# New ranks and later landings in the planner that writes a hybrid decoder layer's instruction order

## The chip, the cores and the metric

The kernel runs on one core of a Trainium2 chip. The metric is the device time in microseconds (us) from the start to the end of one execution; several executions are timed and the median is given. Five engines work beside each other: TensorE (PE in the profile), VectorE (DVE), ScalarE (ACT), GpSimd (POOL) and SyncE (SP), which issues nearly all transfers. Each engine works through its own instructions in the order in which they are written; waits between engines go over semaphores.

## The reference

One layer over 4096 tokens of width 1024, in float32. The input is normalised, scaled and shifted by a conditioning vector, and goes through one input projection that feeds three groups of heads; their gated outputs are joined, projected, normalised and added to the input:

```python
h = _rmsnorm(x, g_pre) * (1.0 + scale[:, None]) + shift[:, None]
proj = h @ w_in
aq, ak, av, ag, rkv, rg, gq, gkk, gv, gg = jnp.split(proj, ...)
attn = _sliding_window_attention(aq, ak, av, sinks) * silu(ag)      # 8 heads, window 128, sinks, ALiBi
rwkv = _rwkv7_mixer(h, rr, rk, rv, ...) * silu(rg)                  # 4 heads, a state of 64 x 64 each
gla  = _gla_mixer(h, gq, gkk, gv, ...) * silu(gg)                   # 4 heads, a state of 32 x 64 each
y = jnp.concatenate([attn, rwkv, gla], axis=-1) @ w_out
return x + gate[:, None] * _rmsnorm(y, g_post)
```

The RWKV group is a recurrence over tokens, `S = S*w + sa*(kk*a) + v*k`, with `sa = -S@kk`. In chunks of 64 tokens it needs, for each chunk and head, the inverse of a triangular 64 x 64 matrix.

## The kernel before

The tokens go in 16 tiles of 256. The work has two phases with a handover between them. Every projection is made of three float16 products (high by high, high by low, low by high parts).

In the first phase each tile passes these stages, whose names are the keys of `LAG`:

- `a` loads and normalises the tile and splits it into `hT` (also stored to DRAM for the second phase);
- `p` makes its projections, PSUM tiles `pv`, `lp`, `zz` (keys, receptances, values) and `gqk`, in a tag `pj` of two banks, and evicts them, `zz` by ACT into `zs` and by DVE into `zb`;
- `w` (the function `stage_d`) makes decays and gates, with `zp`, `gp`, `wps`, `aps`;
- `qa` normalises keys (`np`), makes the products `KB` and `RA` on DVE, the chunk matrices `atp` in PSUM and `AT`, and stores their diagonal blocks of 16 x 16 to DRAM (`adr`);
- `qb` reads them back as `AS`, inverts them row by row on DVE in 15 pairs of `tsc` and `TT`, stores the result (`tdr`) and reads it back as `td` by eight transfers;
- `qc` widens the inverse to 64 x 64 by four bursts of small matmuls (`Xp`, `Xq`, `Xp`, `X2`, the last shown as `X`) into `tf`;
- `v` transposes values (`vp`) and makes the bonus (`bp`); `k` transposes `KB` (`kp`, two bursts) into `BK`;
- `q2` runs the recurrence over the tile's four chunks (`rp`, `up`, `sp`, `yp`) and normalises its output (`ysb`, `yt`);
- `r` is the GLA group (`ktp`, `gap`, `kvp`, `op`, `ot`).

Three further stages run beside them: `l` splits the first phase's weights k, r, v and gqk at the start; `c` reads the second phase's weights piece by piece (`cs`), splits them (`ch`) and stores them to DRAM; `g` makes the output gate.

The second phase has `s` (attention: scores `sc`, softmax, `ovp`), `m` (joins and scales the three groups and splits them into blocks `mtp`) and `p2` (queries, keys and values `qp`, `kp`, `vp`; gates `gp`; and the seven products `op` of the output projection, in a scheme of sums of blocks, whose weights `o` stay in SBUF or come as `ov`). The handover (loads of the second phase's weights, the first tile's attention, the first projections) is written between the phases, outside the planner's lists.

The order is made in two steps. First the stages are generators, run by `emit()` with a coarse model of time: this fixes the program order, the tiles and the buffers. Second, `Order.note` records for each instruction an engine, a modelled duration `occ`, a modelled time to its result `lat`, and what it needs; and `Order.pin`, called once for each phase, is a list scheduler: for the engine that is free first it takes, among the steps that are ready by the model, the one with the lowest `rank`, and ties the engine's instructions together in that order. A rank is the step's number in program order plus an offset:

```python
st.half, st.rank = None, len(self.steps) + self.lag
...
self.model.order.lag = LAG.get(self.model.stage, 0) - self.model.order.urgent
```

`urgent` is 150 around evictions of the second phase (`URGENT`) and 0 in the first. On PE a step of another array shape than the one in use is taken only when no step of that shape is ready, or after it has waited 0.6 us where the shape in use is the full one. A transfer's data are ready `lat` after its issue starts, or later where a shared pipe of 400 GB/s says so.

Of the kernel before, what the change touches and what calls it, by code (L numbers as in the profile page):

```python
# [31 lines left out]
HOP, VL, AL, PL = 0.4, 0.2, 0.2, 0.06  # L32
EXP_TABLE, LN_TABLE = 1, 2
LIFT = {}
LAG = {"l": 150}
URGENT = 150
HOME = {('kp', 'mq'): 'tr', ('cw', 'm'): 'at'}
TILING_WAIT = 0.6
# [27 lines left out]
class Order:  # L66
# [34 lines left out]
    def note(self, eng, name, outs, ins, func, r):  # L101

        st = Step()
# [3 lines left out]
        e, o = st.eng, outs[0]  # L107
# [3 lines left out]
        if e == "PE":  # L111
            f32, lhs = ins[0].dtype == F32, self.region(ins[0])
            n = math.prod(o.shape[1:])
            _, p0, p1, _ = self.region(o)
            rows, cs = (lhs[1] // 32, (lhs[2] + 31) // 32), (p0 // 32, (p1 + 31) // 32)
            rows, cs = [(0, 4) if b - a > 2 else (a, b) for a, b in (rows, cs)]
            mode = (rows[1] - rows[0], cs[1] - cs[0])
            took = n * (2 if f32 else 1) / 2400 + 0.003
            took = max(took, 0.056 if not f32 else 0.0 if mode[1] < 4 else 0.109 if n > 16 else 0.21)
            issue = 0.017 if f32 and mode == (1, 2) else 0.009 if f32 and mode[0] == 1 else 0.007  # L120
            cells = [4 * a + b for a in range(*rows) for b in range(*cs)]
            st.array = (mode, cells, 2 if f32 and name == "matmul" else 1, took, issue)
            st.occ = st.lat = 0.0
        elif e == "SP":
            st.bytes = math.prod(ins[0].shape) * SIZE[ins[0].dtype]
            kb = st.bytes / 1024
            st.occ = 0.47
            st.lat = next((t for k, t in ((8, 2.0), (32, 2.2), (128, 2.8), (256, 3.7), (512, 4.6)) if kb <= k), 5.2)
        elif e == "Activation":
            st.occ = (0.05 if on_psum else 0.093) + 0.093 * (len(ins) - 1) + 0.832e-3 * n  # L130
            st.lat = st.occ + 0.1
            if len(outs) > 1:
                st.occ += 0.187
                st.lat = st.occ + 0.02
            st.table = LN_TABLE if func == AF.Ln else EXP_TABLE if func in (AF.Exp, AF.Tanh) else None
        elif e == "Pool":
            if name == "memset":
                st.occ = 0.06
            elif name == "tensor_copy":
                st.occ = 0.25 if n <= 2 else 0.11 + 0.95e-3 * n  # L140
            elif n <= 8:
                st.occ = 0.33 + 0.165 * n
            else:
                st.occ = 0.42 + 1.5e-3 * n if n <= 512 else 1.85e-3 * n
            st.lat = st.occ + 0.05
        else:
            if name == "tensor_reduce":
                n = math.prod(ins[0].shape[1:])
            fast = name in ("tensor_scalar", "tensor_single_scalar") and not on_psum and o.dtype == F32
            fixed, rate = 0.065 + 0.06 * (cols > 0), 1.04e-3  # L150
            if fast:
                rate = 0.53e-3
            elif name == "transpose":
                fixed = 0.09
            elif name == "tensor_tensor_scan":
                rate = 2.08e-3
            elif name == "memset":
                fixed, rate = 0.05, 0.3e-3
            elif name == "tensor_tensor" and len(o.shape) == 3 and o.shape[2] <= 16 and n > 16:
                fixed, rate = 0.09, 1.55e-3  # L160
            st.occ = fixed + rate * n
            st.lat = st.occ + 0.085
# [70 lines left out]
    def pin(self):  # L233
# [22 lines left out]
        while count < len(steps):  # L256
            e = min((e for e in ENGINES if ready[e]), key=lambda e: max(free[e], min(ready[e].values())))
            now = max(free[e], min(ready[e].values())) + 1e-9
            at = sorted((k for k, t in ready[e].items() if t <= now), key=lambda k: (steps[k].rank, k))
            k = at[0]  # L260
            if e == "PE" and mode is not None and steps[k].array[0] != mode:

                same = [q for q in at if steps[q].array[0] == mode]
                wait = max(now - ready[e][q] for q in at if steps[q].array[0] != mode)
                if same and (mode != (4, 4) or wait < TILING_WAIT):
                    k = same[0]
            if steps[k].port and held > now + SWAP:
                k = next((q for q in at if not steps[q].port), k)
            first = max(free[e], ready[e].pop(k))
            for k in bursts.get(k, [k]):  # L270
                st, t = steps[k], max(first, free[e])
                if e == "PE":
                    m, at, passes, took, issue = st.array
                    if mode is not None and m != mode:
                        t = max(t, max(cells)) + 0.094
                    mode = m
                    t = max(t, max(cells[c] for c in at))
                    for c in at:
                        cells[c] = t + passes * took
                    free[e], st.end = t + issue * passes, t + passes * took + 0.165  # L280
                else:
                    if st.half is not None:
                        was, half[e] = half.get(e, st.half), st.half
                        if was[0] != st.half[0] or None not in (was[1], st.half[1]) and was[1] != st.half[1]:
                            t = max(t, free[e] + 0.115)
                    if st.table is not None and st.table != table:
                        t, table = max(t, free[e] + 1.28), st.table
                    if st.port:
                        t = max(t, held)
                        held = t + st.occ  # L290
                    free[e], st.end = t + st.occ, t + st.lat
                    if st.bytes:

                        pipe = max(pipe, t + 1.7) + st.bytes / 400e3
                        st.end = max(st.end, pipe)
                st.start = t
                if e in last:
                    self.tc.add_manual_dep(
                        st.ins, last[e], mybir.DependencyInfo(mybir.DependencyClass.NoSync, mybir.DependencyReason.DATA))
                last[e], count = st.ins.name, count + 1  # L300
                for q in st.then:
                    to, h = steps[q], head[q]
                    left[h] -= 1
                    at = t if k in to.turn else 0.0
                    if k in to.needs and e != to.eng:
                        at = max(at, st.end + HOP_FROM[e] + HOP_INTO.get(to.eng, 0.0))
                    elif k in to.needs and (e == "SP" or e != "PE" and to.needs[k]):
                        at = max(at, st.end + (0.05 if e == "SP" else 0.03))
                    when[h] = max(when[h], at)
                    if not left[h]:  # L310
                        ready[to.eng][h] = when[h]
# [27 lines left out]
class Lane:  # L339
# [6 lines left out]
    def __getattr__(self, name):  # L346
        f = getattr(self.eng, name)

        def call(*args, **kw):
# [7 lines left out]
            self.model.order.behind = self.model.gate if self.model.stage in ("c", "g") else None  # L357
            self.model.order.lag = LAG.get(self.model.stage, 0) - self.model.order.urgent
            self.model.order.note(self.eng, name, aps[:1] + ([] if accum is None else [accum]),
# [1852 lines left out]
```

## Time and profile before

| what | value |
|---|---|
| median of 3 runs | 1984.49 us (1982.57 to 1984.66) |
| the profiled execution | 1984.65 us, span 1982.8 us |
| PE busy | 1878.0 us (95%) |
| DVE busy | 1425.1 us (72%) |
| ACT busy | 1111.7 us (56%) |
| POOL busy | 369.9 us (19%) |
| granted TensorE clock, mean | 0.989 |

The span runs from the first to the last instruction of the core; the time includes what lies around it. Nearly all instructions are recorded by one helper, so rows of the profile carry its line, L352, and are told apart by the names of what they write and read: `zb<-zz,mu_c,zs` is an instruction that writes zb and reads zz, mu_c and zs. "Idle before" is the time in which an engine did nothing before the instruction, and the name behind the arrow is what ended it. `SPq` is SP's queue of transfer issues.

### The profile page before, as it was taken

The page shows a single profiled execution, that of the slowest core. Times are in us where ns is not written, and L with a number is a line of the kernel's source. Part 1 is how long each engine was busy: PE and PEld are TensorE (multiplying, and loading weights), DVE is VectorE, ACT ScalarE, POOL GpSimd, SP SyncE. Part 2 cuts the span into 40 slices and gives each one's busy share as a digit, 9 for nine tenths or more (in the row PEclk, how much of TensorE's full clock was granted, in tenths as well). Part 3 has the DMA queues.
Part 4 walks back from the last instruction along what each step waited for, and adds up shares of the span by engine and source line. Part 5 has one row for each costly group of instructions (what it writes and reads, how often), then busy time and mean ns, then how long its engine had stood idle before and what let it go on. Part 6 is the DMA issues. An engine that isn't in the chain of part 4 may idle for free.

```text
span 1982.8 us, 59059 instructions
## 1 busy us (share of the span) xinstructions
PE 1878.0 (95%) x24651; PEld 1451.6 (73%) x24651; DVE 1425.1 (72%) x3919; ACT 1111.7 (56%) x2529; POOL 369.9 (19%) x549
## 2 busy tenths in 40 slices
PE   5889999899999999999899999999999999999997
PEld 1667778778777877787777677876778777787783
DVE  4878777887877888877657776667666676666756
ACT  4977877666776677654335443444434444344443
POOL 0623223452322444332200000000000000000001
PEclk8999999999999999999999999999999999999999
DMA  9464444443342434225244433344333434334315
GB/s 376 139 214 141 150 126 132 130 126 110 114 149 76 134 96 122 62 67 162 88 143 145 152 110 113 111 145 124 117 110 111 150 118 123 105 112 153 110 47 182
DMA packets 154261, 257.55 MB, mean 130 GB/s; under 512 B 49026, under 2 KB 100994, under 8 KB 147844
## 3 DMA queue, kind: packets, MB, share of 16 engines
q1 hardware_dynamic: 153844, 253.19, 40.0%
q8 instruction: 195, 3.19, 0.7%
q14 instruction: 78, 0.64, 0.1%
q10 hardware_dynamic: 144, 0.52, 0.1%
HBM read 192.83 MB, written 60.82 MB: 128 GB/s over the span
## 4 chain that ended last, share of the span: by engine, by line
PE 58%; DVE 19%; ACT 9%; DMA 9%; issue 3%; SPq 2%; POOL 1%; DVEq 0%; ACTq 0%; POOLq 0%
PE gp L352 17%; PE op L352 11%; PE zz L352 5%; PE qp L352 5%; PE kp L352 3%; PE pv L352 2%; PE lp L352 2%; PE ovp L352 2%; DVE mtp L352 2%; DVE q L352 2%; DMA AS<-adr 2%; PE gqk L352 2%; PE sc L352 2%; SPq L352 2%; DVE pr L352 1%
## 5 line engine op out<-in xcount | busy, mean ns | idle before, releaser
L352 PEld LDWEIGHTS <-mtp 128*128 128x128 f16 x1344 | 128.7, 98 | 143.4 <-issue 8.1
L352 ACT ACTIVATE pr<-pr,nm,lsc 128x160 f32<-128x160 f32 (+2 forms) x256 | 129.0, 506 | 100.8 <-DVE nm L352 100.8
L352 PE MATMUL op<-o,mtp 128*128 128x512 f16 x768 | 182.2, 379 | 2.6 <-DVE yv L352 2.6
L352 PE MATMUL op<-ov,mtp 128*128 128x512 f16 x576 | 142.2, 379 | 3.1 <-DMA ov<-woscr 2.4
L352 PEld LDWEIGHTS <-hT 128*128 128x128 f16 x1536 | 120.3, 99 | 31.4 <-issue 8.1
L352 DVE SCALAR_TENSOR_TENSOR ag<-ag,gp 128x512 f32<-128x512 f32 x64 | 43.9, 686 | 136.9 <-ACT ag L352 136.9
L352 ACT ACTIVATE ag<-gp,gh 128x512 f32<-128x512 f32 x64 | 43.9, 686 | 156.9 <-PE gp L352 156.8
L352 POOL TENSOR_TENSOR ry<-sy,expo 128x1 f32<-128x1 f32 x30 | 17.7, 608 | 582.9 <-DVE sy L352 582.9
L352 DVE TENSOR_TENSOR yv<-op,yv 128x512 f32<-128x512 f32 x105 | 72.2, 689 | 60.5 <-PE op L352 41.1
L352 PE MATMUL pv<-gvh,hT 128*128 128x272 f16 x512 | 99.5, 288 | 12.8 <-DVE zb L352 6.6
L352 PE MATMUL zz<-hT,rh 128*128 128x256 f16 x512 | 93.9, 277 | 0.4 <-DVE zb L352 0.3
L352 PE MATMUL zz<-hT,kh 128*128 128x256 f16 x512 | 90.7, 274 | 0.0
L352 DVE CUSTOM_DVE_ANT_0 pr<-sc,ab,kept 128x160 f32<-128x160 f32 (+2 forms) x256 | 83.2, 375 | 10.4 <-PE sc L352 10.2
L352 PE MATMUL lp<-hT,Lh 128*128 128x256 f16 x512 | 90.6, 273 | 0.1
L352 PE MATMUL zz<-hT,vh 128*128 128x256 f16 x512 | 89.5, 274 | 0.0
L352 PE MATMUL gp<-hT,q4h 128*128 128x256 f16 x512 | 87.8, 273 | 1.6 <-issue 1.6
L352 PE MATMUL gqk<-hT,gqkh 128*128 128x256 f16 x512 | 88.4, 274 | 0.8 <-DVE zb L352 0.8
L352 PE MATMUL gp<-hT,q3h 128*128 128x256 f16 x512 | 86.7, 273 | 0.0
L352 PE MATMUL qp<-hT,q0h 128*128 128x256 f16 x512 | 86.0, 273 | 0.0
L352 PE MATMUL qp<-hT,q1h 128*128 128x256 f16 x512 | 85.7, 272 | 0.0
L352 PE MATMUL gp<-hT,q5h 128*128 128x256 f16 x512 | 85.5, 273 | 0.0
L352 PE MATMUL gp<-hT,q6h 128*128 128x256 f16 x512 | 85.0, 273 | 0.0
(429 smaller groups left out, 5723.1 us busy)
## 6 DMA issues: line engine op xcount, KB each, us to landing
ov<-woscr SPq DMA_DIRECT2D x96, 512.0 KB, 4.1
xh<-in_x SPq DMA_DIRECT2D x32, 512.0 KB, 4.0
xt<-in_xc SPq DMA_DIRECT2D x16, 1024.0 KB, 8.4
hscr<-hT SPq DMA_DIRECT2D x16, 1024.0 KB, 5.0
hT<-hscr SPq DMA_DIRECT2D x16, 1024.0 KB, 4.8
x<-in_x SPq DMA_DIRECT2D x30, 512.0 KB, 4.2
out<-yv SPq DMA_DIRECT2D x30, 512.0 KB, 2.9
cs<-in_w SPq DMA_DIRECT2D x56, 256.0 KB, 3.5
```

Of the source, the lines that this page charges most:

```text
L352: r = f(*args, **kw)
```

## The change

Three edits in the planner, none in the computation. Fourteen stages get an offset of rank, where one had it before; the modelled landings of transfers become later; and a step on SP that needs an earlier transfer's data is taken to be ready 1.2 us after that landing.

```diff
-LAG = {"l": 150}
+LAG = {"l": 150, "a": -50, "qb": -100, "qc": -200, "k": -150, "c": 170, "p": 130, "v": 130, "r": 120, "w": 60, "q2": 40, "m": -100, "p2": -80, "s": 50}
...
             st.occ = 0.47
-            st.lat = next((t for k, t in ((8, 2.0), (32, 2.2), (128, 2.8), (256, 3.7), (512, 4.6)) if kb <= k), 5.2)
+            st.lat = next((t for k, t in ((8, 2.2), (64, 3.2), (128, 3.4), (256, 4.4), (512, 5.8)) if kb <= k), 7.5)
...
                     elif k in to.needs and (e == "SP" or e != "PE" and to.needs[k]):
-                        at = max(at, st.end + (0.05 if e == "SP" else 0.03))
+                        at = max(at, st.end + (1.2 if e == "SP" else 0.03))
```

The lists of durations and the rule for array shapes stay as they are, and so do program order, tiles and buffers.

## The prediction

> **What bounds the kernel now.** I read the page's first part, then a table of five stretches of the span.
>
> ```profile
> span 1982.8 us, 59059 instructions
> PE 1878.0 (95%) x24651; PEld 1451.6 (73%) x24651; DVE 1425.1 (72%) x3919; ACT 1111.7 (56%) x2529; POOL 369.9 (19%) x549
> 0.00:150.00 150.00, 112.04 (x992) 77.07 (x993) 101.94 (x292) 106.08 (x206) 49.48 (x78) 0.93 0.68 241
> 150.00:950.00 800.00, 769.54 (x12411) 620.49 (x12409) 642.70 (x1920) 561.13 (x1209) 276.44 (x408) 0.99 0.39 120
> 950.00:1020.00 70.00, 63.81 (x1126) 50.69 (x1124) 43.32 (x180) 29.84 (x88) 13.71 (x16) 1.00 0.30 95
> 1020.00:1950.00 930.00, 913.28 (x10044) 695.27 (x10042) 618.43 (x1498) 404.48 (x1010) 24.24 (x42) 1.00 0.38 121
> ```
>
> The columns are length, then busy time and instructions of PE, weight loads, DVE, ACT and POOL, then granted clock, DMA share, GB/s. The stretches are the fill (to 150), the first phase in its stride (to 950), the handover, and the second phase. PE is the bound in both phases, so only time in which PE does nothing, or spends more than the work needs, can be won: 30.5 us idle in 150 to 950 (800 less 769.54), 6.2 in the handover, 16.7 in the second phase. The first phase has 12411+1920+1209+408 = 15948 instructions of the four engines in 800 us, 20 per us; the second 12594 in 930 us, 13.5 per us. An offset of 100 ranks is thus about 5 us of the first phase and 7.4 us of the second (estimates from those rows).
>
> Next, what PE waited for: columns are the waiting instruction, who released it, us in total, times, longest. The first ten rows are of 150 to 985, the next of 0 to 150, the last of 1020 to 1950.
>
> ```profile
> PE ot L352 <- DVE osb L352: 3.4, 3, 1.7
> PE sp L352 <- ACT UV L352: 2.9, 3, 2.3
> PE yt L352 <- POOL ysb L352: 2.9, 1, 2.9
> PE kp L352 <- DVE KB L352: 2.3, 1, 2.3
> PE Xp L352 <- DVE D L352: 2.2, 2, 1.3
> PE X L352 <- DVE Xs L352: 1.7, 1, 1.7
> PE zp L352 <- ACT vg L352: 1.4, 2, 0.8
> PE pv L352 <- DVE kg L352: 1.4, 2, 0.9
> PE up L352 <- DVE rs L352: 1.2, 1, 1.2
> PE atp L352 <- DVE gmin L352: 1.0, 1, 1.0
> PE pv L352 <- DVE zb L352: 6.6, 2, 5.1
> PE sc L352 <- DVE q L352: 6.5, 25, 0.4
> ```
>
> These waits are short and many: PE works through a written order, and a step at its head that the plan expected sooner holds everything behind it. They fall in three classes. Of the inverse and what feeds it (kp, Xp, X, atp): 2.3+2.2+1.7+1.0 = 7.2 us. Of the recurrence (sp, up, yt): 2.9+1.2+2.9 = 7.0. Of stages that the change moves back (ot, zp, pv): 3.4+1.4+1.4 = 6.2.
>
> **The change part by part.** No instruction, transfer, tile or wait is added or removed. What changes is the rank by which the planner picks among ready steps, and how late it believes a transfer's data; so the five written orders (PE, DVE, ACT, POOL, SP) are the only thing that differs.
>
> *Later landings.* Issue to landing, median, from the page and the DMA view:
>
> ```profile
> xt<-in_xc SPq DMA_DIRECT2D x16, 1024.0 KB, 8.4
> xh<-in_x SPq DMA_DIRECT2D x32, 512.0 KB, 4.0
> v<-vscr SPq DMA_DIRECT2D x128, 64.0 KB, 3.8
> AS<-adr SPq DMA_DIRECT2D x32, 64.0 KB, 2.3
> adr<-AT SPq DMA_DIRECT2D x128, 8.0 KB, 1.8
> POOL AS L352 <- DMA AS<-adr: 65.5, 15, 7.4
> ACT ch L352 <- DMA cs<-in_w: 12.0, 5, 5.2
> ACT xh L352 <- DMA xh<-in_x: 10.5, 5, 7.4
> DVE D L352 <- DMA td<-tdr: 6.6, 4, 4.7
> SPq L352 <- DMA tdr<-TT: 20.0, 14, 3.1
> ```
>
> The planner believed 5.2 us for 1024 KB and now 7.5 (8.4 measured), 4.6 and now 5.8 for 512 KB (4.0), 2.8 and now 3.2 for 64 KB (3.8 and 2.3), 2.0 and now 2.2 for 8 KB (1.8). Only the first and the gathered values were told too early by the median; the others are margin for the late ones, and late ones exist: the last five rows (150 to 985, the SP row whole run) are waits of up to 7.4 us for transfers planned earlier. The new 1.2 us from a landing to a dependent issue on SP (0.05 before) answers the last row: SP stood 20 us in 14 waits at the read back of the inverse, with loads queued behind. What it buys is order: ACT, DVE and SP are given other work before the late datum. ACT is busy 561 of 800 us and DVE 643, so a wait there reaches PE only where an eviction stands behind it. I take nothing for it beyond the PE rows of the inverse, whose data come by these transfers; its bounds are 0 and the 6.6 us of D.
>
> *Inverse first* (qc -200, k -150, qb -100, a -50, beside qa at 0). The SP issues of qb (2 AS, 2 tdr, 8 td per tile) and a's three loads pass c's piece loads; POOL's tf copies pass c's subtractions; the matmuls of qc and k pass projections. Nothing of it is longer. With p, r, v and c held 6 us (120 to 170 ranks) back, PE more often has projections left when a step of the inverse is late. I take the inverse class, 7.2 us, as gone, and half of the recurrence class, 3.5 us, since q2 goes back by only 40. Below: at worst neither goes. What is late next is the moved-back class, 6.2 us, which I leave as it is.
>
> The cost is interruptions. One of them, from the timeline of PE (start, length):
>
> ```profile
> 938.36 0.27 PE L352 MATMUL kp<-hT,q2h 128*128 128x256 f16 x1
> 938.57 0.75 PE L352 MATMUL Xp<-D,ATm 32*32 32x32 f32 x64
> 939.25 0.28 PE L352 MATMUL kp<-hT,q2h 128*128 128x256 f16 x1
> 1268.19 2.62 PE kp L352 x24
> ```
>
> Undisturbed, such a matmul takes 2.62/24 = 0.109 us; here 0.21 us pass from the last kp to the first Xp, so a change of array shape costs 0.10 us, some 0.2 us in and out. A tile has 9 bursts that gain rank against projections (four of qc, three of qa, two of k). If one per tile that now stands beside a burst of its own shape is cut loose, that is 13 tiles x 0.2 = 2.6 us; bounds 0 and 9 x 0.2 x 13 = 23.4 us. I take 2.6, since these rows show a burst that interrupts already.
>
> The Trainium skill, TensorEngine Tiling (Array Packing), Key Properties, says that changing the tiling mode drains TensorE, a rule that speaks against this change. The 0.10 us above agrees with it; counted for every burst, the rule would make the sum slower than before, as in the fourth rival.
>
> *Projections, values, gates and weights later.* The evictions of p carry +130 too. Where the cover is gone shows the fill:
>
> ```profile
> 139.78 0.38 PE L352 MATMUL rb<-first,rsx 128*128 128x128 f32 x2
> 145.25 0.39 PE L352 MATMUL pv<-gvh,hT 128*128 128x272 f16 x1 [5.09 <-DVE zb L352]
> 140.29 0.82 ACT L352 ACTIVATE zs<-zz,mu_s 128x256 f32<-128x256 f32 x2
> 139.92 0.88 DVE L352 SCALAR_TENSOR_TENSOR rn<-zb,kkh,rn 128x256 f32<-128x256 f32 x2 [4.08 <-ACT rn L352]
> 143.73 0.68 DVE L352 TENSOR_TENSOR KB<-ta,em 128x512 f32<-128x512 f32 x1
> 144.34 0.87 DVE L352 SCALAR_TENSOR_TENSOR zb<-zz,mu_c,zs 128x256 f32<-128x256 f32 x2
> ```
>
> The last zs was done at 141.11, and zb, which empties the bank, began at 144.34 behind qa's row of products, from 139.92 on; PE stood 5.09 us. In the stride another bank or a small burst covers this (kg cost PE 1.4 us in all), and I cost the delay at nothing there. The weight stage l, behind p by 150 before, is behind it by 20 now, which matters in the fill alone. I leave the fill at 0, bounded by the 6.6 us of zb either way. The conversion stage c goes back 8 us, and its work ends tiles before the phase does: nothing. The handover I leave at 0 too, bounded by its 6.2 us idle.
>
> *Second phase* (m -100, p2 -80, s +50). Scores fall 130 ranks, 9.6 us, behind output products and projections, while the block preparation is pulled up. The sc waits on q, 6.5 us in 25, come of scores that stand directly behind q's eviction; with products ahead of them I take 4 as gone. At worst ovp slides until m is late; the order before has gates and a whole output product behind ovp, so I expect none.
>
> Sum: -7.2 -3.5 +2.6 -4.0 = -12.1 us. The profiled execution took 1984.65 us (span 1982.8 and 1.85 around it), 0.2 above the median 1984.49. Forecast 1984.65 - 12.1 = 1972.5 us.
>
> **Rivals.** First, more is won: with projections kept back, the moved-back class (6.2 us) and the 6.6 us of zb in the fill go as well: 1972.5 - 12.8 = 1959.7. For it: all these waits have the same cause. Against it: those stages are the ones moved back.
>
> Second, nothing changes: PE is busy 96% and 98% of the two strides, every wait is under 3 us, and a new order has new misfits of the same sum: 1984.65.
>
> Third, slower: p's evictions come behind qa's and a's work on DVE (80% busy in the stride) in every tile, as at 139.92 to 144.34. At half of 5.09 us in 13 tiles that is 33 us: 1972.5 + 33 = 2005.6. It decides from 12.1/13 = 0.93 us per tile. Against it: the stride shows only 1.4 us of pv waits now.
>
> Fourth, slower by interruptions: 23.4 in place of 2.6 us: 1993.3.
>
> **How the numbers follow.** Forecast 0.41 (own range 1963 to 1980), more won 0.20, nothing 0.16, evictions 0.16, interruptions 0.07. About 0.2%, 4 us, is what a measurement tells here from no change: faster 0.61, same 0.16, slower 0.23. The range 1950 to 1997 takes in everything but the dear half of the eviction case (about 0.12) and a deeper gain (about 0.05).
>
> **What would show it.** The waits of PE in the first stride: kp, Xp, X and atp gone, sp, up and yt halved, ot, zp and pv as before; sc on q under 3 us; POOL's wait for AS and SP's for tdr shorter. A longer list of pv, zz or gqk behind DVE zb or ACT zs would show the third rival; the same waits but a longer stride, the fourth. The prediction fails if the saved waits come back under other names, which the busy sum of PE in the two strides would tell.

## The result and the profile after

The changed kernel takes 1972.54 us (median of 12 runs, 1966.87 to 1981.63) where the kernel before takes 1986.47 in the runs made beside it: a ratio of 0.9935, with an interval of 0.9922 to 0.9947, so 0.65% faster. One of the twelve executions of the kernel before took 2694.72 us; the ratio and its interval are of the others. The changed kernel's profiled execution took 1972.81 us, of which 1971.0 are the span; that is 11.8 less span than before. The forecast was 1972.5. The sum came out to the microsecond, its terms did not, as the third section shows.

The page of the changed kernel (span, busy time by engine, the instruction queue of the DMA part, the chain of waits by engine):

```profile
span 1971.0 us, 59112 instructions
PE 1875.8 (95%) x24651; PEld 1458.2 (74%) x24651; DVE 1412.5 (72%) x3919; ACT 1118.1 (57%) x2529; POOL 375.2 (19%) x549
...
q8 instruction: 196, 3.21, 0.7%
...
PE 80%; DVE 6%; DMA 5%; ACT 5%; issue 3%; SPq 1%; POOL 1%; DVEq 0%; ACTq 0%; POOLq 0%
```

The same chain of the kernel before:

```profile
PE 58%; DVE 19%; ACT 9%; DMA 9%; issue 3%; SPq 2%; POOL 1%; DVEq 0%; ACTq 0%; POOLq 0%
```

The work is the same, 24651 matmuls. PE is busy 2.2 us less and idle 9.6 us less (1971.0 - 1875.8 = 95.2, before 1982.8 - 1878.0 = 104.8); together the 11.8. The chain that ended last now runs 80% over PE, with 10% in place of 18% over ACT and DMA and 6% in place of 19% over DVE. That is a shift of the chain and not a gain of the same size, as PE's idle time fell by 9.6 us alone. Where the time was won shows in the table of stretches of the changed kernel, with the columns of the prediction:

```profile
0.00:150.00 150.00, 110.11 (x977) 76.18 (x978) 99.27 (x293) 107.11 (x207) 47.88 (x79) 0.93 0.69 244
150.00:950.00 800.00, 780.55 (x12617) 628.37 (x12616) 640.83 (x1936) 564.21 (x1218) 285.08 (x412) 0.99 0.39 119
950.00:1020.00 70.00, 63.56 (x991) 52.49 (x990) 42.36 (x169) 29.67 (x82) 10.95 (x12) 0.95 0.39 129
1020.00:1950.00 930.00, 911.28 (x10028) 696.90 (x10027) 622.34 (x1509) 413.42 (x1014) 27.30 (x44) 1.00 0.39 123
```

PE's idle time falls by 11.0 us in the stride of the first phase (769.54 to 780.55 busy of 800) and rises by 1.9 in the fill, 0.3 in the handover and 2.0 in the second phase; the short end after 1950 makes the rest. The stretches are cut at fixed times and do not hold exactly the same work, so I also follow marks, the starts of certain matmuls in PE's timeline. Of the kernel before, the last projection of the first phase, its last transpose `yt`, and the first `ovp` of the second phase:

```profile
929.88 0.27 PE L352 MATMUL gqk<-hT,gqkl 128*128 128x256 f16 x1
1013.40 0.66 PE L352 MATMUL yt<-first,ysb 128*128 128x128 f32 x4 [2.70 <-POOL ysb L352]
1016.17 1.17 PE L352 MATMUL ovp<-pT,v 32*64 32x160 f32 x46
```

and of the changed kernel:

```profile
930.50 0.28 PE L352 MATMUL gqk<-hT,gqkl 128*128 128x256 f16 x1
1003.24 1.11 PE L352 MATMUL yt<-first,ysb 128*128 128x128 f32 x4 [3.01 <-POOL ysb L352]
1009.95 1.33 PE L352 MATMUL ovp<-pT,v 32*64 32x160 f32 x63
```

The last projection ends no sooner than before. What is won shows behind it: the drain from there to the last `yt` is 72.7 us where it was 83.5. At the last projection, the same number of microseconds has gone by, but more of the inverse and the recurrence, which used to trail behind, is done. From the first `ovp` to the last matmul (1971.4 before, 1959.9 after) the second phase takes 950.0 us, before 955.2.

What PE waited for in the changed kernel (columns as in the prediction: waiting instruction, releaser, total, times, longest). The first eight rows are of 150 to 950, the next three of 0 to 150, the last four of 1020 to 1950:

```profile
PE vp L352 <- DVE zb L352: 3.3, 1, 3.3
PE up L352 <- DVE rs L352: 2.1, 1, 2.1
PE gqk L352 <- DVE zb L352: 1.9, 2, 1.6
PE Xp L352 <- issue: 1.8, 1, 1.8
PE Xq L352 <- DVE Xs L352: 1.7, 2, 1.1
PE kp L352 <- DVE KB L352: 1.7, 1, 1.7
PE Xp L352 <- ACT UV L352: 1.2, 1, 1.2
PE Xp L352 <- DVE AT L352: 1.1, 1, 1.1
...
PE wssp L352 <- ACT gqkh L352: 4.9, 1, 4.9
PE gqk L352 <- DVE zb L352: 4.2, 1, 4.2
PE Xp L352 <- DVE D L352: 2.6, 1, 2.6
...
PE ovp L352 <- issue: 8.4, 4, 2.4
PE gp L352 <- issue: 5.5, 3, 2.1
PE op L352 <- DVE yv L352: 2.4, 1, 2.4
PE kp L352 <- issue: 1.1, 1, 1.1
```

In 150 to 950 the whole list of the changed kernel has 18 rows with 20 waits and 19.4 us, that of the kernel before 26 rows with 34 waits and 29.8 us. A wait is as long as it was, just under 1 us in the mean; there are fewer of them, and most of those of 1 us or more are at other places (`kp` behind `KB` and `up` behind `rs` are in both lists).

### The profile page after: what moved, and what is told of

It is laid out like the page before. It is cut to its first block, busy times and chain, and to the rows that moved or that the text cites. A ratio compares the mean times of both kernels' runs of the same rounds, so it can differ in the third digit from the quotient of the medians.

```text
span 1971.0 us, 59112 instructions
## 1 busy us (share of the span) xinstructions
PE 1875.8 (95%) x24651; PEld 1458.2 (74%) x24651; DVE 1412.5 (72%) x3919; ACT 1118.1 (57%) x2529; POOL 375.2 (19%) x549
## 3 DMA queue, kind: packets, MB, share of 16 engines
q8 instruction: 196, 3.21, 0.7%
## 4 chain that ended last, share of the span: by engine, by line
PE 80%; DVE 6%; DMA 5%; ACT 5%; issue 3%; SPq 1%; POOL 1%; DVEq 0%; ACTq 0%; POOLq 0%
PE gp L352 17%; PE op L352 14%; PE zz L352 8%; PE qp L352 8%; PE pv L352 4%; PE lp L352 4%; PE gqk L352 3%; PE kp L352 3%; PE vp L352 2%; PE ovp L352 2%; PE sc L352 2%; PE atp L352 2%; PE yp L352 1%; PE rp L352 1%; DMA xh<-in_x 1%
## 5 line engine op out<-in xcount | busy, mean ns | idle before, releaser
L352 ACT ACTIVATE xt<-xt,sh,gs 128x256 f32<-128x256 f32 x128 | 70.0, 591 | 30.6 <-DVE xt L352 28.3
```

Of the source, the lines that this page charges most:

```text
L352: r = f(*args, **kw)
```

## The experiments

All were run in five rounds beside the kernel before. The marks are the starts named above, from each kernel's own profiled execution, in us. A mark alone says little below some 3 us: up to 920 us the changed kernel and the one with eight more PE instructions have the same order, and yet at 672 us the second is 3.4 us behind, after 6.8 us at half clock that the first did not have.

| kernel | ratio (95%) | last gqk | last yt | first ovp | last matmul |
|---|---|---|---|---|---|
| before | 1 | 929.9 | 1013.4 | 1016.2 | 1971.4 |
| after | 0.9935 (0.9922 to 0.9947) | 930.5 | 1003.2 | 1009.9 | 1959.9 |
| landings only | 1.0206 (1.0185 to 1.0227) | 943.2 | 1055.0 | 1044.9 | 2015.4 |
| ranks only | 0.9954 (0.9937 to 0.9972) | 931.6 | 1005.6 | 1014.3 | 1960.2 |
| latencies only, no 1.2 us | 1.0200 (1.0187 to 1.0213) | 952.8 | 1050.0 | 1045.2 | 2012.3 |
| ranks mirrored | 1.0632 (1.0605 to 1.0658) | 1019.3 | 1153.8 | 1123.3 | 2104.9 |
| inverse ranks alone | 1.0039 (1.0026 to 1.0052) | 927.4 | 1019.8 | 1011.9 | 1976.7 |
| late ranks alone | 1.0019 (1.0006 to 1.0032) | 934.6 | 1016.9 | 1020.4 | 1972.6 |
| ranks half more | 0.9995 (0.9979 to 1.0011) | 933.2 | 1006.5 | 1015.2 | 1966.5 |
| no second-phase ranks | 0.9987 (0.9974 to 1.0000) | 931.2 | 1003.6 | 1010.5 | 1966.0 |
| weights first | 0.9925 (0.9907 to 0.9943) | 922.5 | 996.9 | 1005.6 | 1961.2 |
| eight more PE instructions | 0.9940 (0.9924 to 0.9956) | 933.4 | 1005.9 | 1012.8 | 1959.7 |
| thirty-two more | 1.0001 (0.9987 to 1.0015) | 931.1 | 1004.0 | 1013.3 | 1971.3 |
| weights first, eight more | 0.9944 (0.9929 to 0.9959) | 923.2 | 1003.7 | 1010.7 | 1962.6 |

### Which edit: landings or ranks

Landings only: the offsets of before in the changed kernel.

```diff
-LAG = {"l": 150, "a": -50, "qb": -100, ...}
+LAG = {"l": 150}
```

> The offsets of rank are undone, the later landings stay. Theory A (ranks win the time): within 0.2% of before, ratio 0.998 to 1.002, with the first stride's tile period at 56 us and sc still waiting some 6 us for q. Rival B (the landings win it): ratio near 0.994, tile period near 55.2 us. Rival C (any new order gains or loses by chance): anything in 0.992 to 1.006.

Ranks only: the landings of before in the changed kernel.

```diff
-            st.lat = next((t for k, t in ((8, 2.2), (64, 3.2), (128, 3.4), (256, 4.4), (512, 5.8)) if kb <= k), 7.5)
+            st.lat = next((t for k, t in ((8, 2.0), (32, 2.2), (128, 2.8), (256, 3.7), (512, 4.6)) if kb <= k), 5.2)
...
-                        at = max(at, st.end + (1.2 if e == "SP" else 0.03))
+                        at = max(at, st.end + (0.05 if e == "SP" else 0.03))
```

> The landings are undone (latencies and the 1.2 us on SP as before), the offsets of rank stay. Theory A: ratio 0.992 to 0.996, tile period near 55.2 us, sc's waits for q gone. Rival B: near 1.000 with a period of 56 us and PE still waiting for the inverse's data.

The ranks alone give 0.9954, the landings alone 1.0206: 40 us slower than before. So the ranks win the time. That the landings alone would cost was in none of the three expectations. With the ranks in place they cost nothing that shows; whether they add the last 0.2% stays open, as the intervals of ranks only and of the whole change overlap.

What the landings do by themselves, from the stretches of landings only (stride, handover) and from the rows of its inverse (`tsc`: shortest, median and longest instruction in ns, start of the first and of the last):

```profile
150.00:950.00 800.00, 756.91 (x11980) 606.54 (x11970) 619.35 (x1841) 548.60 (x1182) 263.83 (x394) 0.99 0.38 118
950.00:1020.00 70.00, 56.17 (x869) 42.98 (x870) 46.90 (x176) 30.27 (x72) 19.15 (x21) 0.85 0.18 59
...
L352 DVE TENSOR_TENSOR tsc<-TT,AS x240: 164/273/1178, 119.8 to 1017.1; 128x16 f32<-128x16 f32 x8, 128x32 f32<-128x32 f32 x8, 128x48 f32<-128x48 f32 x8, 128x64 f32<-128x64 f32 x8
```

and the same row of the kernel before, then of the changed kernel:

```profile
L352 DVE TENSOR_TENSOR tsc<-TT,AS x240: 166/278/1223, 120.6 to 973.2; 128x16 f32<-128x16 f32 x8, 128x32 f32<-128x32 f32 x8, 128x48 f32<-128x48 f32 x8, 128x64 f32<-128x64 f32 x8
```

```profile
L352 DVE TENSOR_TENSOR tsc<-TT,AS x240: 166/278/1148, 120.1 to 964.1; 128x16 f32<-128x16 f32 x8, 128x32 f32<-128x32 f32 x8, 128x48 f32<-128x48 f32 x8, 128x64 f32<-128x64 f32 x8
```

The last step of the inverse of the last tile starts at 1017.1 in place of 973.2, 44 us later, as much as the span is longer (2026.8 against 1982.8). The projections end only 13 us later; the drain behind them grows from 83.5 to 111.8 us, and the handover has 13.8 us idle PE in place of 6.2. My reading is that a chain that crosses DRAM twice per tile, and whose steps are believed ready later, is passed by work that needs no transfer; with offsets that put it first, it is not. In the changed kernel the last inverse is 9 us earlier than before, and the last `yt` 10.2.

How 0.2 to 2.3 us of belief grow to 44 shows when the traces are read tile by tile. I take the distance from the end of a tile's last `gqk` to the start of its last inverse step (`tsc`), in us, and count the tiles from 1 here:

| kernel | tile 1 | tile 4 | tile 8 | tile 12 | tile 16 | mean of 16 |
|---|---|---|---|---|---|---|
| before | 42 | 53 | 50 | 68 | 43 | 53 |
| after | 30 | 44 | 42 | 50 | 33 | 42 |
| landings only | 42 | 57 | 71 | 88 | 74 | 67 |

With the landings alone the inverse falls back behind the projections by some 4 us a tile, up to the twelfth, until it trails by more than a tile's time (some 59 us there). Before, the distance grows too, but to 68. Which decision of the planner starts it was not followed.

Which of the two edits of landings it is: the kernel before with the new latencies alone, without the 1.2 us.

```diff
-            st.lat = next((t for k, t in ((8, 2.0), (32, 2.2), (128, 2.8), (256, 3.7), (512, 4.6)) if kb <= k), 5.2)
+            st.lat = next((t for k, t in ((8, 2.2), (64, 3.2), (128, 3.4), (256, 4.4), (512, 5.8)) if kb <= k), 7.5)
```

> The kernel before with the later latencies alone, without the 1.2 us on SP. If the hop is what made the landings dear (four of them stand in each tile's inverse: 4.6 us of modelled time), this is near before: 1.000 to 1.006, with the last gqk to last yt near 85 us. If the latencies did it: 1.012 to 1.022 and near 110 us, as with both.

1.0200, within the interval of both edits together: the latencies carry the cost, the 1.2 us on SP next to none of it. The loss lies elsewhere, though: here the last projection comes 22.9 us later than before and the drain behind it takes 97.2 us, not the 110 that were expected, and the mean distance of the inverse is 61 us.

### Which ranks, and how much of them

Ranks mirrored: the ten offsets of the first phase with their signs turned, so that projections, values, gates and weights go first and the inverse later.

```diff
-LAG = {"l": 150, "a": -50, "qb": -100, "qc": -200, "k": -150, "c": 170, "p": 130, "v": 130, "r": 120, "w": 60, "q2": 40, ...}
+LAG = {"l": 150, "a": 50, "qb": 100, "qc": 200, "k": 150, "c": -170, "p": -130, "v": -130, "r": -120, "w": -60, "q2": -40, ...}
```

> The changed kernel with the offsets of the first phase's ten moved stages turned to their opposites: the inverse later, projections and values earlier; landings and second phase as changed. Theory A: slower than before, the stride's period above 57 us, PE's waits for kp, Xp and X over 10 us: ratio 1.003 to 1.02. Rival C (the direction is of no matter): 0.994 to 1.000.

6.3% slower, by far the largest effect of the study and more than the 0.3 to 2% expected; 2.1% of it is what the new landings cost without ranks. Its stride (150 to 950):

```profile
150.00:950.00 800.00, 720.66 (x10776) 577.42 (x10775) 579.20 (x1691) 512.77 (x1111) 236.75 (x361) 0.95 0.35 108
```

PE is idle 79 us there and its clock is granted at 0.95. The distance of the inverse is 98 us in the mean. Of the waits, 24.8 us are of the inverse, 15.7 of the recurrence and 35.1 of the rest, so the evictions of the projections suffer as well as the inverse. Not any reordering would have won: the direction decides.

The two halves of the first-phase offsets, each in the changed kernel. Inverse ranks alone:

```diff
-LAG = {... "a": -50, "qb": -100, "qc": -200, "k": -150, "c": 170, "p": 130, "v": 130, "r": 120, "w": 60, "q2": 40, ...}
+LAG = {... "a": -50, "qb": -100, "qc": -200, "k": -150, ...}
```

> The changed kernel without the six offsets that move projections, values, gates, recurrence, GLA and the weight conversion back (c, p, v, r, w, q2 at 0; l, a, qb, qc, k, m, p2, s and the landings as changed). Theory A (what counts is the distance of the inverse from the projections, whichever is moved): most of the gain, 0.994 to 0.999, and from the last gqk to the last yt about 75 to 80 us (83.5 before, 72.7 changed, 111.8 with landings alone). Rival (holding the filler back is what counts): above 1.005, with that stretch over 90 us.

Late ranks alone:

```diff
+LAG = {... "c": 170, "p": 130, "v": 130, "r": 120, "w": 60, "q2": 40, ...}
```

> The changed kernel without the four offsets that pull the inverse forward (a, qb, qc, k at 0). Theory A: some of the gain, 0.996 to 1.005. Rival (holding the filler back is what counts): 0.993 to 0.996, as the changed kernel.

1.0039 and 1.0019. Neither is faster than before, but both hold the new landings and have to be read against 1.0206 (they also have the offsets of the second phase): either half brings back most of what the landings cost, and only both bring the kernel below. That fits a rank as a difference, but only roughly. The mean distance of the inverse is 53 us with the inverse ranks alone, as before, and 47 with the late ranks alone, against 42 with both and 67 with none: in the main the time follows this distance. It does not follow the distance of the ranks, which is 200 between `qc` and `p` in the slower of the two halves and 130 in the faster. The inverse ranks alone came out between their two expectations (1.0039, with a drain of 92.4 us, which is in the rival's range), the late ranks alone as expected.

Ranks half more: the ten offsets times 1.5.

```diff
+LAG = {"l": 150, "a": -75, "qb": -150, "qc": -300, "k": -225, "c": 255, "p": 195, "v": 195, "r": 180, "w": 90, "q2": 60, ...}
```

> The changed kernel with the first phase's ten offsets half as large again (a -75, qb -150, qc -300, k -225, c 255, p 195, v 195, r 180, w 90, q2 60), l, the second phase and the landings as changed. From the last gqk to the last yt the kernels so far took 134 us (mirrored), 112 (landings alone), 92 and 82 (one half of the ranks), 73 (changed). If distance goes on winning: under 68 us there and a ratio of 0.985 to 0.992. If it is used up, because nothing but the last tile's own inverse is left in that stretch: 70 to 78 us and 0.992 to 1.000, with more of PE's waits on zz, gqk and pv.

0.9995: the gain is gone. Its largest wait in 150 to 985:

```profile
PE gqk L352 <- DVE zb L352: 8.6, 6, 3.0
```

The wait of `gqk` for the eviction `zb`, 1.9 us in the changed kernel, is 8.6 now: the projections are held so far back that their own evictions are the misfit, as in the prediction's third rival. The inverse comes no closer for it: its mean distance is 43 us, where the changed kernel has 42. Of the 6.6 us by which its span is longer than the changed kernel's (1977.6 against 1971.0), 5.3 stand at the first `ovp`.

### The second phase

No second-phase ranks: the changed kernel without `m`, `p2` and `s`.

```diff
-LAG = {..., "m": -100, "p2": -80, "s": 50}
+LAG = {...}
```

> The changed kernel without the three offsets of the second phase (m, p2, s). By my sum the second phase gave 4 us: 1976 us, ratio 0.9955, with the sc waits of 6.5 us back. By the trace of the changed kernel, where the longer issue waits of ovp and gp ate the gain: 1972 to 1974, no difference to the changed kernel beyond 2 us.

0.9987 against 0.9935 with them. The first phases are alike (last `yt` at 1003.6 and 1003.2). From the first `ovp` to the last matmul this kernel takes 955.5 us, the kernel before 955.2, the changed one 950.0. So the three offsets bring 5.5 us in the profiled executions; by the ratios it is 0.5% of 1986 us, some 10 us, more than either expectation. One part shows in the waits of this kernel in 1020 to 1950:

```profile
PE sc L352 <- DVE q L352: 6.5, 25, 0.4
PE ovp L352 <- issue: 6.3, 5, 1.6
```

The 25 waits of `sc` for `q` are there again, 6.5 us as in the kernel before; with the offsets all of them are gone. Yet PE's idle time behind the first `ovp` hardly differs, 19.5 us without the offsets and 18.7 with them, as `issue` takes in the changed kernel what `sc` gave up (next but one section). The 5 us stand in PE's busy time, 936.4 us against 931.6. The matmuls of `op` right before an `sc` show most of it: without the offsets it takes 0.274 us in the mean from their start to the next (90 of them, idle time not counted), with them 0.216. The profile counts a wait from the modelled end of the matmul before it, 0.38 us behind its start for `op`, while the next one follows after 0.22 where nothing waits; so a short wait costs more than its row says.

### The fill

Weights first: `l`, which splits the first phase's weights, at -60 rather than 150.

```diff
-LAG = {"l": 150, "a": -50, ...}
+LAG = {"l": -60, "a": -50, ...}
```

> The changed kernel with the first phase's weight stage l at -60 in place of 150, ahead of projections as of most else. If the fill lost its time because the weights of r, v and gqk are split late, the waits of wssp for gqkh (4.9 us) and of gqk for zb (4.2) go, the second tile's pv starts near 96 instead of 104, and the whole gains 4 to 8 us on the changed kernel: ratio 0.989 to 0.992. If ACT and DVE bound the fill whatever their order, no difference: 0.993 to 0.995.

In the changed kernel the projections of tile 2 (the third `pv`) begin at 149.9 where they began at 145.3 before. Here they begin at 139.5. Of PE's waits in the fill of this kernel, the one of `gqk` for `zb` is shorter (4.2 in the changed kernel), and the wait for `gqkh` (4.9) has no row, one for `rh` in its place:

```profile
PE wssp L352 <- ACT rh L352: 6.0, 1, 6.0
...
PE gqk L352 <- DVE zb L352: 1.7, 1, 1.7
```

The last projection ends 8.0 us and the last `yt` 6.3 us earlier than in the changed kernel, but the last matmul is 1.3 us later, and the ratio, 0.9925, cannot be told from 0.9935. The second phase, whose order is the same, took 955.6 us from its first `ovp` where it took 950.0. What is won in the first phase is lost again in the second: that led to the last three runs.

### What the second phase depends on besides its order

PE's waits that the profile puts down to `issue` rose in the second phase: `ovp` 3.7 to 8.4, `gp` 2.6 to 5.5, `kp` from none to 1.1 (before, there was 0.4 for `qp`). The profile of the changed kernel lists an instruction queue, q8: 196 packets, 3.21 MB, so 16.4 KB each, and 2 x 24651 / 256 = 193 pages. I count all instructions of PE in the trace: weight loads, matmuls and the some 300 semaphore instructions between them. In both kernels these waits come at counts whose remainder by 256 is 193 or 194, and each of the second phase ends 1.2 to 1.6 us behind the end of a packet of q8. They begin within some 4 us of the start of a burst of `ovp`, some 190 small matmuls with as many weight loads in 2.9 us. If PE waits there for its next page of instructions, some more PE instructions ahead of the second phase move its bursts against the pages, and change the time without a change of its order.

Eight more PE instructions: the transpose `fp` of the changed kernel, which is done once, at 920 us, and whose result is overwritten by the same each time, runs five times: four more weight loads and four more matmuls. (The two expectations count one transpose fewer than the runs have, and places in a page from a point 134 instructions earlier than the text below does.)

```diff
-        PE.transpose(fp[:1, :P], gmin, ident)
+        for _ in range(5):
+            PE.transpose(fp[:1, :P], gmin, ident)
```

> The changed kernel with the one transpose of the handover's flag (fp) done four times instead of once: 8 more PE instructions (a weight load and a matmul each) before the second phase, nothing else meant. In ten traces the issue waits of the second phase begin at one remainder of the PE instruction's number by 256, and their length goes by where in such a page the ovp burst (384 instructions in 2.9 us) begins: at 49 to 55 it is 2.0 to 2.6 us, at 56 to 66 1.0 to 1.6, at 241 to 247 1.1 to 2.8, at 248 to 254 0.5 to 1.8, at 106 to 204 none. Moved by 8, ovp begins at 57, 121, 185 and 249 instead of 49, 113, 177 and 241. Page theory: issue waits of the second phase fall from 15 us to 5 to 9 and fewer of them halve the clock; the whole gains 5 to 12 us: ratio 0.987 to 0.991. Rival (the waits belong to the order of work or to the ov transfers beside them): no change, 0.992 to 0.995.

Thirty-two more PE instructions: the same loop with `range(17)`, sixteen more transposes, between 920 and 933 us.

> The same with sixteen transposes: 32 more PE instructions... less the two that were there, 30 more, so ovp begins at 79 to 81, 143 to 145, 207 to 209 and 15 to 17. Page theory: waits of 1.1 to 1.4, none, none to 1.4 and 2.4 to 2.6 per four tiles: 13 to 17 us in the phase, no gain: ratio 0.991 to 0.996. If any extra instructions helped, it would be as the run before.

Eight more change nothing that can be told (0.9940). Their `issue` waits are 7.8 + 6.4 + 1.1 = 15.3 us, where 5 to 9 were expected: the finer expectation, read off the waits of the old order, was wrong. Thirty-two more take the whole gain back (1.0001), which no expectation had. The order of the second phase is the same; that of the last first-phase work and of the handover is not quite, and 3.4 us of the loss are there already at the first `ovp`. Matched from the end, matmul by matmul, this kernel is 3.5 us behind the changed one at 1072 us and 12.3 behind at 1765, in steps at the bursts of `ovp`. Its waits of 1020 to 1950, and one burst in PE's timeline:

```profile
PE ovp L352 <- issue: 17.6, 7, 3.1
PE gp L352 <- issue: 0.7, 2, 0.5
...
1687.82 2.85 PE L352 MATMUL ovp<-pT,v 32*64 32x128 f32 x187
1693.79 0.43 PE L352 MATMUL ovp<-pT,v 32*64 32x32 f32 x5 [3.12 <-issue]
```

`issue` now costs 17.6 + 0.7 = 18.3 us, and 0.4 in a row for `vp`, where it cost 8.4 + 5.5 + 1.1 = 15.0. In the changed kernel the bursts from 1120 to 1810 us begin 43, 107, 171 and 235 instructions behind the last such count, turn by turn, and PE waits 0, 1.5 to 2.1, 2.2 to 2.4 and 0 us in and right behind them; in this one they begin 74, 138, 202 and 10 behind, and it waits at most 0.5, 2.4 to 3.1, 2.0 to 2.6 and 0.

All fourteen traces together decide it. They have 210 bursts of 192 matmuls. Each of the 103 that begin 102 to 226 behind such a count has an `issue` wait in it or right behind it, of 0.4 to 3.1 us; of the 96 that begin 0 to 71 or 228 to 254 behind, none has; of the 11 between 72 and 101, six have, of at most 0.6. So whether PE waits goes with the place in the page. How long does not go by the place alone: a burst at 108 waited 0.4 in the order of the kernel before, one at 107 up to 2.1 in the changed kernel. Most of the rest of the 8.8 us are half-clock windows (last section), of which this kernel has four between the first `ovp` and 1765 us where the changed one has two, up to 1.7 us each.

Weights first and eight more: both edits.

> The kernel with the weight stage at -60 and the eight more PE instructions. The weight stage at -60 alone won 8 us to the last gqk and lost 5.6 us again in the second phase to issue waits of 16 us and a clock halved for longer. Page theory: both add, 1957 to 1965 us, ratio 0.984 to 0.989. Rival: as with the weight stage alone, 0.991 to 0.994.

0.9944. The hope that the better fill would show at another alignment was not met: its first `ovp` comes at 1010.7, no sooner than the changed kernel's. From the last `gqk` to the last `yt` it takes 80.5 us where weights first takes 74.4, and one wait for `issue` there takes 4.4. No version beat the changed kernel by more than can be told.

## Why the prediction was right or wrong

**The number.** -12.1 us were forecast, -11.8 came in the profiled span. That they agree so closely is luck: the changed kernel's own executions spread over 14.8 us, and the terms behind the sum were off in both directions and cancelled. The waits of the named classes gave less, others gave more, the fill lost, and a page effect that I had not seen added 8.3 us of waits in the second phase, twice its own term.

**The inverse and the recurrence (-7.2 and -3.5).** That the inverse has to go ahead of the projections is shown by the mirrored ranks and by the distances: with the inverse 98 us behind PE idles 79 us in the stride, at 53 us (before) 30.5, at 42 us (after) 19.4. Which waits would go was right in part. Those of `Xp` for `D`, `X` for `Xs`, `atp` and `sp` are gone, `kp` has 1.7 of its 2.3 us left, and `up` has more than it had. I put PE's waits of 150 to 950 together by the stage of the waiting instruction, whatever released it. The inverse (`kp`, `Xp`, `Xq`, `X`, `atp`, `np`) had 10.9 us and has 8.4; its rows came back as `Xq` and `Xp` for other data. Of both sums some are `issue` waits, 3.3 and 2.1 us, at the same place of a page as those of the second phase; the 2.5 us of `Xp` among them were not in the prediction's rows, and its reasons for the ranks do not reach them. The recurrence had 6.4 and has 3.7 (with the 2.9 of `yt`, which came between 950 and 985 and are gone, it gave 5.6). The projections, gates and GLA, the class "moved back", which I left as it is, had 12.3 and has 7.3, though `vp` waits for `zb` anew and `gqk` longer (the `ot` of the last tile has 2.8 us more between 950 and 985, in the handover, whose idle time stayed the same). So in the stride the two terms, -10.7 as put, gave -2.5 and -2.7, and the step "what is late next is the moved-back class, 6.2 us, which I leave as it is" failed: half of the gain, -5.0, came from there. That holding these stages back gave their data time to arrive, as the first rival had it, fits this and is not shown apart from the rest; the rival's other half, the fill, went the other way.

**Interruptions (+2.6).** Up to 985 us PE changes its array shape 596 times where it changed 578 times, but by then it has also done more of the work. Over the whole run it is 650 against 647, and the changes from or to the full shape, of which the prediction's was one, are 582 against 546. At 0.10 us each these counts give 0.3 to 3.6 us. The size of the term fits; the fourth rival (23.4) is refuted, and with it the count of every burst as an interruption.

**Landings (0, bounds 0 and 6.6).** The step failed twice. Its bound had only a gain, and alone the edit costs 40 us. And what it was to buy came in part, without reaching PE, as the prediction held possible. The waits for transfers in 150 to 985 and SP's own of the changed kernel, against the rows of the prediction, then three rows of ranks only and one of the kernel before:

```profile
POOL AS L352 <- DMA AS<-adr: 71.3, 13, 10.6
ACT ch L352 <- DMA cs<-in_w: 3.3, 2, 1.7
DVE D L352 <- DMA td<-tdr: 0.4, 1, 0.4
ACT xh L352 <- DMA xh<-in_x: 0.3, 1, 0.3
SPq L352 <- DMA tdr<-TT: 8.1, 11, 1.3
SPq L352 <- DVE TT L352: 100.8, 15, 20.2
...
ACT xh L352 <- DMA xh<-in_x: 7.7, 4, 4.4
DVE D L352 <- DMA td<-tdr: 0.3, 1, 0.3
SPq L352 <- DVE TT L352: 107.1, 12, 18.6
...
SPq L352 <- DVE TT L352: 61.8, 14, 20.3
```

D's 6.6 us are 0.4 now, `xh`'s 10.5 are 0.3, `ch`'s 12.0 are 3.3, SP's for `tdr` 20.0 are 8.1. POOL's for `AS` did not fall. SP stands longer at the step before its landing, 100.8 us for `TT` where it stood 61.8. Ranks only has D's 0.3 and 107.1 for `TT` as well, so those two came with the ranks; it has 7.7 for `xh` and 17.5 for `tdr`, so most of the fall of these two is owed to the landings. None of these is a wait of PE. The cost came by the way a modelled latency has in a list: it delays the chain that crosses DRAM against all work that does not, and so changes the order of whole tiles, as the distances tile by tile show. The prediction took it for margin at the place of the transfer.

**The fill (0).** It costs 4.6 us at the start of tile 2. The sentence that `l`, now only 20 ranks behind `p`, matters in the fill alone was the right one; I left it unpriced. Weights first shows it: tile 2 starts 10.4 us earlier, the last projection 8.0.

**Evictions behind qa (third rival, 33 us).** It did not come at these offsets: `gqk` and `vp` wait 1.9 + 3.3 us for `zb` in the stride, against a point of decision of 12.1. At offsets one half larger it begins to show, 8.6 us in `gqk` alone.

**The handover (0).** By idle time it is right, 6.4 us for 6.2. But the gain becomes visible just here, as a drain that is 10.8 us shorter.

**The second phase (-4.0).** -5.5 us against the same kernel without the offsets, and the waits named went: `sc` on `q` from 6.5 to none, not only to under 3. Not foreseen were that each of them also cost busy time, about 5 us in all, and 8.3 us more of `issue` waits, which took back the idle time. What this term is worth without them could not be measured: the same order took 950.0, 958.0 and 946.9 us from the first `ovp` on as it is, with 32 and with 8 more PE instructions.

## What to carry to other kernels

In a list schedule for a pipeline over tiles, look for the longest chain of a tile that leaves the chip's main engine (here twice through DRAM and 30 small steps on DVE), give it the lower ranks, and take a modelled latency as a rank too: raising it moved the chain back and cost 2% until ranks brought it forward again. Size such offsets by trying both signs and more than one size, since the misfits that go and the ones that come are not the ones a list of waits names. A gain under 1% in an order is of the size of its accidents with instruction pages and clock windows; before ascribing it to an idea, move the whole order by some tens of instructions and time it again.

## What the runs showed of the hardware

**Instructions can run out.** The waits above, up to 4.4 us long, come at one place of every 256 instructions of PE, when dense bursts use them up at 187 matmuls with their loads in 2.85 us, some 130 a microsecond. In the fourteen traces PE has 150 waits for `issue`; all stand at remainder 193 or 194, and 149 end 1.2 to 1.6 us behind the end of a packet of the instruction queue. The pages' number and size are shown; that PE waits for the page is inferred from the place, from the packets and from what moving by 32 instructions did. The Trainium skill, Runtime: NRT & Kernel Launch, Instruction fetch mechanics, says that instructions are streamed in blocks of 16 KiB, 256 instructions, and that crossing one is mostly hidden. The size agrees with 16.4 KB a packet. "Mostly hidden" agrees by the count, as 11 of some 193 crossings of the changed kernel have such a wait; behind dense bursts it does not hold, and those 11 leave PE idle for 17.4 us, 15.0 of them in the second phase.

**Half the clock after less than a window of idling.** Around one of those waits, in PE's timeline of the changed kernel and in three stretches of it:

```profile
1253.97 0.43 PE L352 MATMUL ovp<-pT,v 32*64 32x32 f32 x22 [2.41 <-issue]
...
1251.80:1255.20 3.40, 1.23 (x30) 1.11 (x30) 0.16 (x1) 0.84 (x4) 0.00 (x0) 0.99 0.32 129
1255.20:1258.60 3.40, 3.40 (x18) 2.41 (x17) 2.67 (x4) 2.20 (x5) 0.00 (x0) 0.50 0.02 5
1258.60:1262.00 3.40, 3.40 (x33) 3.04 (x32) 0.00 (x0) 0.00 (x0) 0.00 (x0) 1.00 0.00 0
```

PE is idle 2.2 of 3.4 us, and for the next 3.4 us the granted clock is 0.50: 18 matmuls in place of 33, so the wait of 2.4 us costs some 1.6 us more. Between 150 and 1950 this happened three times before (after 1.7 to 2.3 us idle of 3.4) and nine times after (1.8 to 2.7); the mean clock is 0.985 in place of 0.989. The idle time does not decide alone: before, a stretch of 3.4 us from 970.8 on with 1.9 us idle was followed by the full clock. Six more such windows at up to 1.7 us are up to 10 us, nearly what the change won (an estimate from these counts). So a new order that has fewer waits but some long ones pays for them again, and the spread of the runs goes with it in the main: the changed kernel's shortest run, 1966.87 us, had a clock of 0.986, its longest, 1981.63, one of 0.981. The Trainium skill, TensorE: Matmul & The Clock Gate, Part 1: The HAM clock gate, gives a free-running window of about 3.4 us and a clock at half or full, and has it fall to half after at least one idle window. The length and the half agree with these rows; here 1.7 to 2.7 us of idling within 3.4 were enough.

**The size of such accidents.** Sixteen more transposes between 920 and 933 us, which put the first `ovp` 3.4 us later, cost 12.7 us by the medians (1985.2 against 1972.54), as much as the whole change had won. In the profiled executions 3.4 us of it are there at the first `ovp`, and 3.9 are more `issue` waits behind it (18.8 us against 14.9).
